# DeltaNet in a streaming encoder layer: the two tiles of a pair share one chain of small passes for norms and factors, and one for the output norm

## The chip, the cores and the metric

The kernel runs on one core of one Trainium2 chip. A core has five engines with a queue each, worked off in order: PE (TensorE, matmuls and transposes; its weight loads are listed as PEld), DVE (VectorE), ACT (ScalarE), POOL (GpSimd) and SP (SyncE, which here issues the DMAs). The metric is the device time of one execution in microseconds, as the median of the runs.

## The reference

One inference step of one encoder layer, for 2,048 new frames of one stream and for 16 frames each of eight running streams: 2,176 frames or 17 tiles of 128, the last of which (tile 16) is the sample tile. An input projection feeds three mixers: band attention, a gated DeltaNet and an S5 state space model. Their outputs go through an output projection and a feed-forward network, each with a layer norm. Only the DeltaNet (4 heads of 64) is touched. For q and k of each frame and head it needs reciprocal norms, from them six factors, a solve and a recurrence in chunks of 64 frames, and an RMS norm of the output:

```python
conv = jax.nn.silu(conv.astype(f32) + lp['b_conv_b'].astype(f32))
qb, kb, vb = jnp.split(conv, 3, axis=-1)
qb = l2_normalize(qb.reshape(bsz, t_len, B_HEADS, B_HEAD_DIM))
kb = l2_normalize(kb.reshape(bsz, t_len, B_HEADS, B_HEAD_DIM))
...
ob, s_new = gated_delta_rule(qb, kb, vb, g, beta, s0)
gate = jax.nn.silu(gate_b.astype(f32).reshape(bsz, t_len, B_HEADS, B_HEAD_DIM))
ob = ob * lax.rsqrt(jnp.mean(ob * ob, -1, keepdims=True) + RMS_EPS) * lp['b_norm_w'].astype(f32) * gate
```

## The kernel before

The first part, `mix`, runs three streams side by side. `project1` and `project2_all` are the projections: matmuls into the PSUM tile `pps`, each product in three passes (L65 to L67) of values split into a high and a low part (`xh`, `xl` for x, `wh`, `wl` for weights; the split is one copy on ACT, L60, and one subtraction on DVE, L61). `deltanet` and `s5` are the two small mixers. They are generators, and `mix` draws a step of the one or the other at a set pace. What results is a program order; the framework's scheduler then sets the order of each engine's queue from it, and hands out buffers. After `mix` come attention, the output projection and the feed-forward network.

`deltanet` goes through the tiles in pairs: (0,1) to (10,11), then the sample tile 16 alone, then (12,13) and (14,15). For each tile `b_pre` does the convolution with its SiLU (six blocks of features in `s2`, with three passes L512 and one L515 each on DVE), transposes q, k and v on PE (L528, L535), squares and sums q and k (L532), and takes the reciprocal root of the eight sums of a frame by a bit trick and three Newton steps (`rsqrt`, twelve passes of 128x8 on DVE: L343 to L350, tiles `bnt`, `bny`, `bnh`, `bns`, `bnz`). Six more passes (L544 to L549) form F, the factors of q and k. With F come `qkn` on DVE (L572) and `qdkb` on POOL (L574), `kdec` and the right-hand side R; PE transposes `qkn` (L583) and `qdkb` (L587), ACT copies them (`qknT`, `qdT`, `kbT`), and PE forms the scores (L601, into `at` and `qkT` by L603 on DVE).

For both tiles of a pair at once `b_inverse` inverts the 16x16 diagonal blocks on DVE (30 passes on `tp` and `Ti`, L625 and L627) and sends the result through memory (`tD`) into the tile `TU`. Then, tile by tile, `b_solve` (L649, L661, L669), `b_rec` (L686 to L702; two chunks, each by way of DVE) and `b_out`: square on POOL (L770), sum (L772), L773 and a second `rsqrt` of 128x4 (tiles `ont` to `onz`), `osq` (L775), two transposes on PE (L786) into the PSUM tile `brs`, and the gate (L788). `brs` has a single buffer, which the recurrence uses too; `bps`, for the transposes and scores, has two.

Of the kernel before, what the change touches and what calls it, by code (L numbers as in the profile page):

```python
# [9 lines left out]
F32 = mybir.dt.float32  # L10
# [4 lines left out]
OP = mybir.AluOpType  # L15
AX = mybir.AxisListType
# [25 lines left out]
class K:  # L42
# [88 lines left out]
    def mix(self, upto):  # L131
# [10 lines left out]
        with ExitStack() as es:  # L142
            dense = self.project1(es)
            next(dense)
            self.s5_setup()
            for _ in range(5):
                next(dense)
            self.parts_done = 1
            self.b_consts(bes)
            self.b_pools(bes)  # L150
            due = 0.0
            for i, _ in enumerate(dense):
                if i in (5, 11):
                    self.parts_done += 1
                due += PACE1 if i < 12 else PACE1B
                while due >= 1:
                    next(deltanet)
                    due -= 1
        with ExitStack() as es:
            self.merge((self.project2_all(es), 1.0), (deltanet, PACE_B), (self.s5(), PACE_C))  # L160
# [5 lines left out]
    def deltanet(self):  # L166

        gates = -1

        def ready(t):  # L170
            return self.parts_done > min(t // 6, 2)

        for t in [0, 2, 4, 6, 8, 10, 16, 12, 14]:
            n = 1 if t == 16 else 2
            while not ready(t + n - 1):
                yield 0.1
            if gates < min(t // 6, 2):
                gates += 1
                self.b_gates(gates)
            blk = self.bw.tile([32 * n, 16, 16], F32, name="blk", tag="blk", bufs=2)  # L180
            st = []
            for i in range(n):
                st.append(self.b_pre(t + i, blk, i))
                yield 1
            TU = self.b_inverse(st, blk)
            for x, (T, U) in zip(st, TU()):
                self.b_solve(x, T, U)
                o = self.bw.tile([128, 1, 4, 64], F32, name="o", tag="o", bufs=2)
                if t == 16:
                    self.b_rec_sample(x, o)  # L190
                else:
                    self.b_rec([x], o)
                self.b_out(x["t"], 1, o)
                yield 1
        self.nc.sync.dma_start(self.A["o_sp"], self.S)

    def evac(self, dst, src, scale=None):
# [273 lines left out]
    def t2(self, name, tag="pa"):  # L471
        return self.bw.tile([128, 4, 128], F32, name=name, tag=tag, bufs=5 if tag == "pa" else 1)

    def b_pre(self, t0, blk, bi):

        nc, A = self.nc, self.A
        V, mm = nc.vector, nc.tensor.matmul
        n = 1
        sam = t0 == 16
        bw, bk, bp = self.bw, self.bk, self.bp  # L480
        T = n * 128
# [5 lines left out]
        for f in range(6):  # L487
            fr = slice(f * 128, (f + 1) * 128)
            if sam:
# [5 lines left out]
                o = s2[:, f].rearrange("p (b t) -> p b t", t=16)  # L495
            else:
# [12 lines left out]
                o = s2[:, f]  # L509
# [8 lines left out]
        elif t0 + n == 16:  # L518
            nc.sync.dma_start(A["o_cvp"], cv[:, :, 0])
        qk = bw.tile([128, n, 8, 64], F32, name="qk", tag="qk", bufs=2)  # L520
        ss = bw.tile([128, n * 8], F32, name="ss", tag="ss", bufs=2)
        R = []
        for i in range(n):
            t = t0 + i
            ts = slice(i * 128, (i + 1) * 128)
            ps = bp.tile([128, 512], F32, name="bps", tag="b", bufs=2)
            for f in range(4):
                nc.tensor.transpose(ps[:, f * 128:(f + 1) * 128], s2[:, f, ts], self.ident)  # L528
            nc.scalar.copy(qk[:, i], ps.rearrange("p (h d) -> p h d", h=8))
            sq = self.t2("sq").rearrange("p a (b d) -> p (a b) d", d=64)  # L530
            nc.scalar.activation(sq, ps.rearrange("p (h d) -> p h d", h=8), AF.Square)
            V.tensor_reduce(ss[:, i * 8:(i + 1) * 8], sq, AX.X, OP.add)  # L532
            ps = bp.tile([128, 512], F32, name="bps", tag="b", bufs=2)
            for f in range(2):
                nc.tensor.transpose(ps[:, f * 128:(f + 1) * 128], s2[:, 4 + f, ts], self.ident)  # L535
            r = bk.tile([128, 4, 128], F32, name="R", tag="R")
            V.tensor_tensor(r[:, :, 0:64], ps[:, 0:256].rearrange("p (h d) -> p h d", h=4),
                            self.hbeta[:, t].unsqueeze(2).to_broadcast([128, 4, 64]), OP.mult)
            R.append(r)
        V.tensor_scalar(ss, ss, 4e-6, None, OP.add)  # L540
        rn = self.rsqrt(bw, ss, n * 8, "bn").rearrange("p (t h) -> p t h", h=8)
        F = bw.tile([128, n, 6, 4], F32, name="F", tag="F", bufs=2)
# [4 lines left out]
        V.tensor_tensor(F[:, :, 3], F[:, :, 1], self.beta[:, tt], OP.mult)  # L547
        V.tensor_tensor(F[:, :, 4], F[:, :, 3], self.egc[:, tt], OP.mult)
        V.tensor_tensor(F[:, :, 5], F[:, :, 1], self.kd[:, tt], OP.mult)  # L549
        st = []  # L550
        for i in range(n):
            t = t0 + i
# [206 lines left out]
        for p in range(2):  # L759
            nc.sync.dma_start(A["o_ss"][:, p], Sc[p])  # L760

    def b_out(self, t0, n, o):

        nc = self.nc
        V = nc.vector
        bw, bp = self.bw, self.bp
        T = n * 128
        of = o.rearrange("p t h e -> p (t h) e")
        sq = bw.tile([128, n * 4, 64], F32, name="osq", tag="po", bufs=4)
        nc.gpsimd.tensor_tensor(sq, of, of, OP.mult)  # L770
        ms = bw.tile([128, n * 4], F32, name="ms", tag="ms", bufs=2)
        V.tensor_reduce(ms, sq, AX.X, OP.add)  # L772
        V.tensor_scalar(ms, ms, 1.0 / 64, 1e-6, OP.mult, OP.add)  # L773
        rn = self.rsqrt(bw, ms, n * 4, "on")
        V.tensor_tensor(sq, of, rn.unsqueeze(2).to_broadcast([128, n * 4, 64]), OP.mult)  # L775
        g = bw.tile([128, 2, T], F32, name="gt", tag="po", bufs=4)
        gsrc, gs = self.at(self.gT, t0)
        gs = slice(gs.start, gs.start + T)
        nc.sync.dma_start(g, gsrc[:, gs].rearrange("(f p) t -> p f t", p=128))
        th = bw.tile([128, 2, T], F32, name="gth", tag="po", bufs=4)  # L780
        nc.scalar.activation(th, g, AF.Tanh, scale=0.5)
        V.scalar_tensor_tensor(g, th, 1.0, g, OP.add, OP.mult)
        ps = self.brp.tile([128, 512], F32, name="brs", tag="r")
        for f in range(2):
            for i in range(n):
                nc.tensor.transpose(ps[:, f * T + i * 128:f * T + (i + 1) * 128],  # L786
                                    sq[:, i * 4 + 2 * f:i * 4 + 2 * f + 2].rearrange("p a e -> p (a e)"), self.ident)
        V.scalar_tensor_tensor(th, ps[:, 0:2 * T].rearrange("p (f t) -> p f t", f=2), self.nw, g, OP.mult, OP.mult)  # L788
        nc.sync.dma_start(self.mixT[512:768, t0 * 128:t0 * 128 + T].rearrange("(f p) t -> p f t", p=128), th)
# [1145 lines left out]
```

## Time and profile before

| | |
|---|---|
| median of the runs | 2846.88 us (2844.42 to 2847.21, three runs) |
| the profiled execution | 2848.35 us, its span 2846.6 us |
| PE, PEld | 96%, 85% of the span busy |
| DVE, ACT, POOL | 68%, 46%, 36% |
| mean granted clock | 0.991 |
| DeltaNet's part of the span | about 130 to 760 us |

Each row of the profile is read against the engine's queue: an engine works its list in order, so a late operand holds everything behind it. A wait is put down to the instruction that released it. The page's busy shares are means over stages with different limits, so the tables by stretch matter more than they do.

### The profile page before, as it was taken

The page shows a single profiled execution, that of the slowest core. Times are in us where ns is not written, and L with a number is a line of the kernel's source. Part 1 is how long each engine was busy: PE and PEld are TensorE (multiplying, and loading weights), DVE is VectorE, ACT ScalarE, POOL GpSimd, SP SyncE. Part 2 cuts the span into 40 slices and gives each one's busy share as a digit, 9 for nine tenths or more (in the row PEclk, how much of TensorE's full clock was granted, in tenths as well). Part 3 has the DMA queues.
Part 4 walks back from the last instruction along what each step waited for, and adds up shares of the span by engine and source line. Part 5 has one row for each costly group of instructions (what it writes and reads, how often), then busy time and mean ns, then how long its engine had stood idle before and what let it go on. Part 6 is the DMA issues. An engine that isn't in the chain of part 4 may idle for free.

```text
span 2846.6 us, 46363 instructions
## 1 busy us (share of the span) xinstructions
PE 2739.7 (96%) x16685; PEld 2405.9 (85%) x16685; DVE 1947.2 (68%) x4949; ACT 1307.0 (46%) x2714; POOL 1037.4 (36%) x914
## 2 busy tenths in 40 slices
PE   8999999989989899999999999999999999999998
PEld 8988888867777677788889998989999988998897
DVE  7587888798653788878755555566556557676676
ACT  3554554343355778612334433454434335444443
POOL 0010111232221232122354454445544553676674
PEclk9999999999999999999999999999999999999999
DMA  5734445555457652156622211253222224422321
GB/s 183 208 106 118 116 114 125 151 147 155 146 147 244 207 168 61 51 199 203 231 88 65 84 60 60 74 207 119 74 74 90 89 67 165 155 91 94 119 87 55
DMA packets 293437, 355.55 MB, mean 125 GB/s; under 512 B 85699, under 2 KB 218647, under 8 KB 292887
## 3 DMA queue, kind: packets, MB, share of 16 engines
q1 hardware_dynamic: 293206, 352.59, 39.6%
q8 instruction: 131, 2.15, 0.3%
q14 instruction: 100, 0.81, 0.1%
HBM read 280.25 MB, written 74.89 MB: 125 GB/s over the span
## 4 chain that ended last, share of the span: by engine, by line
PE 71%; DVE 12%; DMA 6%; issue 4%; ACT 3%; POOL 3%; SPq 1%; DVEq 0%; ACTq 0%; POOLq 0%
PE fdp L66 8%; PE fdp L67 8%; PE fdp L65 8%; PE pps L66 3%; PE pps L67 3%; PE pps L65 3%; PE wops L65 2%; PE wops L67 2%; PE wops L66 2%; PE fupv L67 2%; PE fupv L65 2%; PE fupv L66 2%; PE fupz L67 2%; PE fupz L65 2%; PE fupz L66 2%
## 5 line engine op out<-in xcount | busy, mean ns | idle before, releaser
L1570 POOL TENSOR_TENSOR wu<-wur,wu 128x512 fp32r<-128x512 f32 x308 | 416.9, 1357 | 600.6 <-ACT wu L1569 599.6
L1693 DVE TENSOR_TENSOR fy<-fy,fdp 128x512 f32<-128x512 f32 x500 | 341.1, 685 | 255.8 <-PE fdp L67 255.6
L65 PE MATMUL fdp<-wdh,hh 128*128 128x512 f32 x1020 | 397.8, 391 | 1.6 <-DVE fy L1693 1.1
L67 PE MATMUL fdp<-wdh,hl 128*128 128x512 f32 x1020 | 397.3, 389 | 1.1 <-DVE hl L1643 1.1
L66 PE MATMUL fdp<-wdl,hh 128*128 128x512 f32 x1020 | 397.2, 389 | 0.8 <-DVE wdl L61 0.8
L1569 ACT CAST wu<-wur 128x512 fp32r<-128x512 f32 x308 | 189.5, 617 | 427.1 <-DMA wur<-in_w_upL 173.5
L65 PE MATMUL pps<-xh,wh 128*128 128x384 f32 (+2 forms) x800 | 280.4, 352 | 11.7 <-ACT xh L60 10.4
L66 PE MATMUL pps<-xl,wh 128*128 128x384 f32 (+2 forms) x800 | 279.9, 350 | 2.1 <-DVE xl L61 2.1
L67 PE MATMUL pps<-xh,wl 128*128 128x384 f32 (+2 forms) x800 | 277.6, 348 | 0.1
L65 PEld LDWEIGHTS fdp<-wdh,hh 128*128 128x128 f32 x1020 | 191.4, 188 | 42.0 <-DVE fy L1693 2.8
L67 PEld LDWEIGHTS fdp<-wdh,hl 128*128 128x128 f32 x1020 | 191.5, 188 | 41.8 <-DVE hl L1643 2.0
L66 PEld LDWEIGHTS fdp<-wdl,hh 128*128 128x128 f32 x1020 | 191.5, 188 | 39.0 <-DVE wdl L61 1.1
L1643 DVE TENSOR_TENSOR hl<-fre,hh 128x384 fp32r<-128x384 f32 (+1 forms) x180 | 145.4, 809 | 83.9 <-ACT hh L1642 83.0
L60 ACT CAST wdh<-wdr 128x1024 fp32r<-128x1024 f32 x92 | 96.6, 1051 | 204.4 <-PE fdp L67 202.7
L65 PEld LDWEIGHTS pps<-xh,wh 128*128 128x128 f32 x800 | 152.1, 191 | 24.9 <-ACT xh L60 12.8
L61 DVE TENSOR_TENSOR wl<-wr,wh 128x512 fp32r<-128x512 f32 (+1 forms) x152 | 107.2, 714 | 87.0 <-ACT wh L60 84.5
L66 PEld LDWEIGHTS pps<-xl,wh 128*128 128x128 f32 x800 | 152.1, 190 | 13.8 <-DVE xl L61 5.1
L67 PEld LDWEIGHTS pps<-xh,wl 128*128 128x128 f32 x800 | 152.1, 190 | 11.4 <-issue 1.8
L61 DVE TENSOR_TENSOR wdl<-wdr,wdh 128x1024 fp32r<-128x1024 f32 x92 | 131.6, 1436 | 11.0 <-ACT wdh L60 10.9
L60 ACT CAST wh<-wr 128x512 fp32r<-128x512 f32 (+1 forms) x152 | 92.4, 619 | 79.8 <-DMA wr<-in_w_inA 35.0
L1638 ACT ACTIVATE fre<-fre,ld_b_up 128x384 f32<-128x384 f32 (+1 forms) x144 | 86.0, 597 | 65.3 <-DVE fre L1647 43.0
L1229 ACT ACTIVATE P<-P,st 128x640 f32<-128x640 f32 (+4 forms) x128 | 97.2, 760 | 30.5 <-DVE st L1226 29.8
(577 smaller groups left out, 7250.7 us busy)
## 6 DMA issues: line engine op xcount, KB each, us to landing
wdr<-in_w_dnL SPq DMA_DIRECT2D x96, 512.0 KB
wur<-in_w_upL SPq DMA_DIRECT2D x88, 512.0 KB
wr<-in_w_inA SPq DMA_DIRECT2D x70, 512.0 KB
TU<-tD SPq DMA_DIRECT2D x34, 256.0 KB
y<-in_x SPq DMA_DIRECT2D x17, 512.0 KB
x<-y SPq DMA_DIRECT2D x17, 512.0 KB
fxr<-x SPq DMA_DIRECT2D x17, 512.0 KB
fy<-x SPq DMA_DIRECT2D x17, 512.0 KB
```

The source lines that it names most:

```text
L60: nc.scalar.copy(hi, src)
L61: nc.vector.tensor_tensor(lo, src, hi.bitcast(F32), OP.subtract)
L65: mm(out, lh, rh, start=first, stop=False, **kw)
L66: mm(out, lh, rl, start=False, stop=False, **kw)
L67: mm(out, ll, rh, start=False, stop=last, **kw)
L1229: self.nc.scalar.activation(x, x, AF.Exp, scale=-1.0, bias=st[:, q:q + 1], accum_out=st[:, 2 + q:3 + q])
L1569: self.nc.scalar.copy(hi, src)
L1570: P.tensor_tensor(lo, src, hi.bitcast(F32), OP.subtract)
L1638: nc.scalar.activation(r, src, AF.Relu, bias=self.bu[:, c * 2 + i:c * 2 + i + 1])
L1643: V.tensor_tensor(hl, r, hh.bitcast(F32), OP.subtract)
L1693: V.tensor_tensor(y, y, ps[x], OP.add)
```

## The change

`b_pre` is cut in three. `b_conv` does the convolution, the transposes and the sums of squares of one tile and writes its eight sums into its half of a shared tile `ss`. `b_factors` runs once for the pair, on 16 columns: one `rsqrt` and one set of six passes for F. The rest of `b_pre` then runs for each tile with its slice of F. In the same way `b_square` sums the squares of a tile's output into its half of a shared `ms`, `b_root` takes one reciprocal root for the pair, and `b_out` follows for both tiles after the second recurrence. A pair still yields four times, at other places. The sample tile goes through the same functions alone.

```diff
             blk = self.bw.tile([32 * n, 16, 16], F32, name="blk", tag="blk", bufs=2)
-            st = []
+            st, qr = [], []
+            ss = self.bw.tile([128, n * 8], F32, name="ss", tag="ss", bufs=2)
             for i in range(n):
-                st.append(self.b_pre(t + i, blk, i))
-                yield 1
+                qr.append(self.b_conv(t + i, ss[:, i * 8:(i + 1) * 8]))
+                if i < n - 1:
+                    yield 1
+            F = self.b_factors(t, n, ss)
+            for i in range(n):
+                st.append(self.b_pre(t + i, *qr[i], F[:, i:i + 1], blk, i))
+                if i < n - 1 or n == 1:
+                    yield 1
             TU = self.b_inverse(st, blk)
-            for x, (T, U) in zip(st, TU()):
+            os_ = []
+            ms = self.bw.tile([128, n * 4], F32, name="ms", tag="ms", bufs=2)
+            for i, (x, (T, U)) in enumerate(zip(st, TU())):
                 self.b_solve(x, T, U)
                 o = self.bw.tile([128, 1, 4, 64], F32, name="o", tag="o", bufs=2)
                 if t == 16:
                     self.b_rec_sample(x, o)
                 else:
                     self.b_rec([x], o)
-                self.b_out(x["t"], 1, o)
-                yield 1
+                os_.append((o, self.b_square(o, ms[:, i * 4:(i + 1) * 4])))
+                if i < n - 1:
+                    yield 1
+            rn = self.b_root(n, ms)
+            for i, (o, sq) in enumerate(os_):
+                self.b_out(t + i, 1, o, sq, rn[:, i * 4:(i + 1) * 4])
+            yield 1
...
-    def b_pre(self, t0, blk, bi):
+    def b_conv(self, t0, ss):
...
-        ss = bw.tile([128, n * 8], F32, name="ss", tag="ss", bufs=2)
...
+        return qk, R
+
+    def b_factors(self, t0, n, ss):
+
+        V, bw = self.nc.vector, self.bw
         V.tensor_scalar(ss, ss, 4e-6, None, OP.add)
         rn = self.rsqrt(bw, ss, n * 8, "bn").rearrange("p (t h) -> p t h", h=8)
...
+        return F
+
+    def b_pre(self, t0, qk, R, F, blk, bi):
...
-    def b_out(self, t0, n, o):
+    def b_square(self, o, ms):
+        sq = self.bw.tile([128, 4, 64], F32, name="osq", tag="po", bufs=4)
+        of = o.rearrange("p t h e -> p (t h) e")
+        self.nc.gpsimd.tensor_tensor(sq, of, of, OP.mult)
+        self.nc.vector.tensor_reduce(ms, sq, AX.X, OP.add)
+        return sq
+
+    def b_root(self, n, ms):
+        self.nc.vector.tensor_scalar(ms, ms, 1.0 / 64, 1e-6, OP.mult, OP.add)
+        return self.rsqrt(self.bw, ms, n * 4, "on")
+
+    def b_out(self, t0, n, o, sq, rn):
...
-        sq = bw.tile([128, n * 4, 64], F32, name="osq", tag="po", bufs=4)
-        nc.gpsimd.tensor_tensor(sq, of, of, OP.mult)
-        ms = bw.tile([128, n * 4], F32, name="ms", tag="ms", bufs=2)
-        V.tensor_reduce(ms, sq, AX.X, OP.add)
-        V.tensor_scalar(ms, ms, 1.0 / 64, 1e-6, OP.mult, OP.add)
-        rn = self.rsqrt(bw, ms, n * 4, "on")
         V.tensor_tensor(sq, of, rn.unsqueeze(2).to_broadcast([128, n * 4, 64]), OP.mult)
```

The scheduler makes new queues of it. Three places follow; a number behind a name tells its buffers apart, and code lines behind the change are shifted (L528 is now L541, L583 is L610).

DVE, factors of the pair (12,13). Before, tile 12 (`qkn_7813`) had them to itself, and its scores (`at_7836`) came before the sums of tile 13 (`ss_8053`):

```order
L549 TENSOR_TENSOR F_7796<-F_7796,b4_kd_1398 128x4
L572 TENSOR_TENSOR qkn_7813<-qk_7762,F_7796 128x512
L548 TENSOR_TENSOR F_7796<-F_7796,b4_egc_1397 128x4
L577 TENSOR_TENSOR kdec_7818<-qk_7762,F_7796 128x256
L603 TENSOR_TENSOR at_7836<-bps_7838,DT_7803 128x2x64
L603 TENSOR_TENSOR qkT_7837<-bps_7838,DM_7804 128x2x64
L603 TENSOR_TENSOR at_7836<-bps_7849,DT_7803 128x2x64
L603 TENSOR_TENSOR qkT_7837<-bps_7849,DM_7804 128x2x64
L537 TENSOR_TENSOR R_8066<-bps_8063,b4_hbeta_1394 128x4x64
L532 TENSOR_REDUCE ss_8053<-sq_8060 128x8
```

Now F is 2x4 wide and both tiles follow it (`qkn_7746` is tile 12, `qkn_7807` tile 13), with convolution passes of tile 14 (`s2_8394`) around:

```order
L565 TENSOR_TENSOR F_7729<-F_7729,b4_beta_1393 128x2x4
L567 TENSOR_TENSOR F_7729<-F_7729,b4_kd_1398 128x2x4
L599 TENSOR_TENSOR qkn_7746<-qk_7493,F_7729 128x512
L566 TENSOR_TENSOR F_7729<-F_7729,b4_egc_1397 128x2x4
L604 TENSOR_TENSOR kdec_7751<-qk_7493,F_7729 128x256
L604 TENSOR_TENSOR kdec_7812<-qk_7696,F_7729 128x256
L599 TENSOR_TENSOR qkn_7807<-qk_7696,F_7729 128x512
L526 SCALAR_TENSOR_TENSOR s2_8394<-cin_8423,ld_b_cw_1358,s2_8394 128x128
```

So tile 12's `qkn` moved behind the sums of both tiles, and tile 13's directly behind it.

PE, the same pair. Before, tile 13's transposes (`s2_7996`) came after tile 12's scores, and tile 13's own `qkn` 43 projection matmuls later:

```order
L786 MATMUL brs_7534<-ld_c_ident_92,osq_7506 128x128 x2
...
L583 MATMUL bps_7823<-ld_c_ident_92,qkn_7813 128x128 x4
L587 MATMUL bps_7829<-ld_c_ident_92,qdkb_7815 128x128 x4
...
L528 MATMUL bps_8054<-ld_c_ident_92,s2_7996 128x128 x4
...
L535 MATMUL bps_8063<-ld_c_ident_92,s2_7996 128x128 x2
...
L583 MATMUL bps_8113<-ld_c_ident_92,qkn_8103 128x128 x4
L587 MATMUL bps_8119<-ld_c_ident_92,qdkb_8105 128x128 x4
```

Now tile 13's transposes (`s2_7640`) stand ahead of the sample tile's output (`osq_7237`), and the two tiles' `qkn` six projection matmuls apart:

```order
L541 MATMUL bps_7697<-ld_c_ident_92,s2_7640 128x128 x4
L548 MATMUL bps_7706<-ld_c_ident_92,s2_7640 128x128 x2
...
L818 MATMUL brs_7264<-ld_c_ident_92,osq_7237 128x128 x2
...
L610 MATMUL bps_7756<-ld_c_ident_92,qkn_7746 128x128 x4
L614 MATMUL bps_7762<-ld_c_ident_92,qdkb_7748 128x128 x4
...
L610 MATMUL bps_7817<-ld_c_ident_92,qkn_7807 128x128 x4
...
L614 MATMUL bps_7823<-ld_c_ident_92,qdkb_7809 128x128 x4
```

So tile 13's transposes moved up by 50 projection matmuls, tile 12's `qkn` down by 8.

DVE, the splits `xl` of the first x of `project2_all`, which PE needs for its next product. Before, the factor chain of tile 14 (`bnz_8785`, `bns_8784`) ran between them:

```order
L61 TENSOR_TENSOR xl50_8614<-xr_8615,xh50_8613 128x512
L625 TENSOR_TENSOR tp_8155<-blk_7699,Ti_8154 64x48
L350 SCALAR_TENSOR_TENSOR bnz_8785<-bns_8784,bnz_8785 128x8
L959 TENSOR_TENSOR WB_9119<-st1_428,pr_400 128x256
L627 TENSOR_TENSOR Ti_8154<-Ti_8154,tp_8155 64x12x4
L348 TENSOR_TENSOR bns_8784<-bnz_8785 128x8
L963 TENSOR_TENSOR ZC_9117<-ZC_9117,tz_9118 128x544
L625 TENSOR_TENSOR tp_8155<-blk_7699,Ti_8154 64x55
L349 TENSOR_TENSOR bns_8784<-bns_8784,bnh_8783 128x8
L512 SCALAR_TENSOR_TENSOR s2_8950<-cin_8952,ld_b_cw_1358,s2_8950 128x128
```

Now it is the convolution of tile 15 (`s2_8549`):

```order
L61 TENSOR_TENSOR xl50_8299<-xr_8300,xh50_8298 128x512
L652 TENSOR_TENSOR tp_7859<-blk_7429,Ti_7858 64x28
L529 SCALAR_TENSOR_TENSOR s2_8549<-th_8588,s2_8549 128x128
L654 TENSOR_TENSOR Ti_7858<-Ti_7858,tp_7859 64x2x14
L1010 TENSOR_TENSOR Kt_8497<-Kt_8497,ld_s5_dI_367 16x2x16
L526 SCALAR_TENSOR_TENSOR s2_8549<-cin_8591,ld_b_cw_1358,s2_8549 128x128
L652 TENSOR_TENSOR tp_7859<-blk_7429,Ti_7858 64x15
L526 SCALAR_TENSOR_TENSOR s2_8549<-cin_8601,ld_b_cw_1358,s2_8549 128x128
L654 TENSOR_TENSOR Ti_7858<-Ti_7858,tp_7859 64x15
L526 SCALAR_TENSOR_TENSOR s2_8549<-cin_8591,ld_b_cw_1358,s2_8549 128x128
```

So between the splits small passes of 8 columns left, and convolution passes of 128 columns and more of the inverse moved up.

## Rows read from the trace of the kernel before

**Rows 1.** The page, part 1: busy time, share and instructions of each engine.
```profile
PE 2739.7 (96%) x16685; PEld 2405.9 (85%) x16685; DVE 1947.2 (68%) x4949; ACT 1307.0 (46%) x2714; POOL 1037.4 (36%) x914
```

**Rows 2.** Busy time of each engine by stretch; first the stretch and its length.
```profile
core 0: us, PE busy (x) PEld busy (x) DVE busy (x) ACT busy (x) POOL busy (x), PEclk, DMA share, GB/s
200.00:300.00 100.00, 96.45 (x692) 84.72 (x692) 81.05 (x326) 46.35 (x119) 13.82 (x16) 1.00 0.39 109
...
500.00:560.00 60.00, 58.20 (x460) 51.75 (x458) 43.60 (x151) 23.98 (x63) 11.97 (x26) 1.00 0.52 146
560.00:586.00 26.00, 25.68 (x158) 20.13 (x159) 18.94 (x62) 6.54 (x15) 9.34 (x22) 1.00 0.32 113
586.00:634.00 48.00, 35.65 (x261) 27.94 (x258) 45.23 (x158) 25.18 (x62) 19.28 (x26) 0.89 0.59 164
634.00:700.00 66.00, 64.58 (x460) 52.76 (x460) 60.55 (x200) 23.11 (x52) 18.07 (x28) 1.00 0.54 152
700.00:760.00 60.00, 56.25 (x333) 43.57 (x332) 38.69 (x112) 18.87 (x39) 8.60 (x15) 0.97 0.45 131
```

**Rows 3.** DVE's groups by shape, 0 to 800 us: count, busy us, mean ns.
```profile
L512 DVE SCALAR_TENSOR_TENSOR s<-cin,ld_b_cw,s 128x128 f32<-128x128 f32 x288 | 100.4, 365 | 3.5 <-ACT s L510 2.4
...
L548 DVE TENSOR_TENSOR F<-F,b_egc 128x4 f32<-128x4 f32 x17 | 10.4, 613 | 0.1
L349 DVE TENSOR_TENSOR bns<-bns,bnh 128x8 f32<-128x8 f32 x51 | 8.5, 166 | 0.3
L349 DVE TENSOR_TENSOR ons<-ons,onh 128x4 f32<-128x4 f32 x51 | 8.5, 166 | 0.1
```

**Rows 4.** DVE in order of time: start us, duration us, line, operation.
```profile
374.28 0.33 DVE L512 SCALAR_TENSOR_TENSOR s<-cin,ld_b_cw,s 128x128 f32<-128x128 f32 x1
374.54 0.15 DVE L544 TENSOR_SCALAR F<-bnz 128x4 f32<-128x4 f32 x1
374.61 0.15 DVE L545 COPY F<-bnz 128x4 f32<-128x4 f32 x1
...
375.77 1.01 DVE L548 TENSOR_TENSOR F<-F,b_egc 128x4 f32<-128x4 f32 x1
```

**Rows 5.** PE's waits from 0 to 560 us: total us, times, longest.
```profile
PE brs L786 <- DVE Ti L627: 2.7, 3, 1.5
PE bps L583 <- DVE qkn L572: 2.5, 3, 1.3
PE bps L587 <- POOL qdkb L574: 2.0, 6, 1.0
...
PE bps L583 <- DVE F L548: 0.6, 1, 0.6
```

**Rows 6.** Busy time from the sample tile's last update to the last split.
```profile
578.00:623.00 45.00, 36.48 (x247) 29.88 (x246) 40.76 (x149) 20.75 (x48) 17.12 (x23) 0.89 0.50 139
```

**Rows 7.** PE in order of time: two projection matmuls.
```profile
590.13 0.34 PE L65 MATMUL pps<-xh,wh 128*128 128x384 f32 x1
590.31 0.34 PE L66 MATMUL pps<-xl,wh 128*128 128x384 f32 x1
```

**Rows 8.** PE's waits from 586 to 634 us.
```profile
PE bps L535 <- DVE s L515: 3.8, 1, 3.8
PE bps L587 <- POOL qdkb L574: 2.2, 2, 2.0
PE bps L528 <- DVE qkT L603: 1.7, 1, 1.7
PE bps L601 <- ACT kbT L590: 1.3, 2, 0.8
```

**Rows 9.** Busy time from 600 to 620 us.
```profile
600.00:620.00 20.00, 15.67 (x60) 11.37 (x60) 19.18 (x56) 9.43 (x18) 9.29 (x11) 0.74 0.67 191
```

**Rows 10.** The chain that ended last, at the last pair's inverse.
```profile
698.51 3.63 DMA tD<-Ti
702.20 3.08 DMA TU<-tD
```

More of the change, by code (lines that the diff above doesn't have):

```diff
@@ L549, in b_pre @@
         V.tensor_tensor(F[:, :, 5], F[:, :, 1], self.kd[:, tt], OP.mult)
+        return F
+    def b_pre(self, t0, qk, R, F, blk, bi):
+        nc = self.nc
+        V, mm = nc.vector, nc.tensor.matmul
+        n = 1
+        sam = t0 == 16
+        bw, bk, bp = self.bw, self.bk, self.bp
         st = []
```

## The prediction

> **What bounds the kernel now.** I read the page first, then busy time by stretch, then who waits for whom on PE and on DVE, then DVE's instructions in order of time. The page [rows 1] shows PE busy for 96% of the span; no other engine is above 85%. So a change of DVE's work is worth only what PE idles for it. The table by stretch [rows 2] says where that is. From 200 to 560 us PE is busy 96 to 97% while DVE has work for 73 to 81% of the time: PE bounds it, and DVE's passes lie beside matmuls. From 586 to 634 us it is the other way round: DVE 45.23 of 48 us, PE 35.65, so PE idles 12.4 us and waits for DVE. After it, PE is at 98%, and from 700 to 760 us at 94%. Only DeltaNet's stretch, about 130 to 760 us, is touched. Behind it PE's order is word for word the old one: the last 9,703 of its 13,017 listed rows agree, only with other line numbers. I count that tail as a pure shift.
>
> **What goes.** A pair of tiles ran two factor chains (19 instructions: L540, twelve in `rsqrt`, six for F) and two output chains (13: L773 and twelve). Now it runs one of each: 32 fewer per pair, 256 for the eight pairs; the sample tile, alone, keeps its 32. Width costs nothing that the rows can show: the 8-wide and the 4-wide pass both last 166 ns [rows 3]. The price of one is the distance between starts, not its duration: where independent passes follow each other, they start 70 ns apart though each lasts 0.15 us [rows 4]. With a little for dependent ones I take 75 ns, and 256 x 0.075 = 19 us of DVE's queue. By durations it would be 256 x 0.166 = 42 us; the starts are the nearer row, since what follows can begin then. The Trainium skill (VectorE: DVE Perf Modes, section The DRAIN you can't avoid) says that the next operation does not start until the pipe is empty; by that the 42 us would count, and the rows at 374.54 and 374.61 do not agree. The one exception stands in the rows too: L548, a four-wide pass, lasts 1.01 us at 375.77 and 613 ns in the mean [rows 3, 4], because POOL reads for `qdkb` just then. One such pass per pair goes, a half us each.
>
> **What it is worth, in time order.** The sum is made against the profiled execution, 2848.35 us (its span 2846.6); it stands 1.5 us above the median of the runs, 2846.88.
>
> (a) Before 560 us the passes are covered by matmuls; if that cover went, the whole 19 us would be on the path. What is not covered is PE's waits at the ends of these chains: 2.7 us where the output transpose (L786) comes, 2.5 us for `qkn`, 2.0 us for `qdkb`, 0.6 us for F: 7.8 us [rows 5]. (The first is put down to `Ti`, which stands beside the output chain in DVE's queue.) One chain of two goes, so 3.9 us; but the one that stays waits for the second tile, so I take **-3.0** (ends 0 and -7.8).
>
> (b) The stretch where DVE bounds. The point that lets PE go on is the last of the eight splits `xl` of the first x of `project2_all`. I count DVE's list from the sample tile's last state update to that split: 148 rows become 147, but others. Out go 37 small passes (37 x 0.075 = 2.8 us), one `qkn` (0.6) and one collision of L548 (0.5). In come 20 passes of the convolution of tile 15 (20 x 0.3 = 6.0, between 0.26 us from its start to the next at 374.28 us [rows 4] and its mean of 365 ns [rows 3]), 15 of the block inverse (15 x 0.13 = 2.0) and S5 passes of 0.8 us. Net +4.9 on 40.76 us, in a piece that took 45 us [rows 6]: DVE idled 4.2 us there, mostly for the transposes and scores of tiles 12 and 13, and now has convolution passes for that time. So the split would end 45.7 us after the start instead of 45, and the start itself comes earlier: 12 projection matmuls fewer stand ahead of it on PE, 0.18 us from start to start [rows 7], 2.1 us. Together **-1.5** (ends -4.9 with the idle time wholly used and less work in front, +4.9 if neither helps). Of PE's waits in this stretch [rows 8], 2.2 us for POOL's `qdkb` and 1.3 us for `kbT` fall behind or beside that split; DVE has tile 15's convolution behind it there already, and I let **-2** of them go (0 to -3.5). The 3.8 and 1.7 us on the transposes of tile 14 are inside the DVE path counted before; they move to x, they do not go twice.
>
> (c) The granted clock is 0.74 between 600 and 620 us [rows 9], that is some 10 us at 1.2 instead of 2.4 GHz, around the waits of 1.7 and 3.8 us; 5.2 us of full clock. PE waits for DVE for much of it, so I take **-1** (0 to -5.2).
>
> (d) Right after the split the new order packs the solve of tile 13, the recurrence of tile 12 and the scores of tile 14 with hardly a projection matmul between, where seven stood before. PE idles 1.4 us from 634 to 700 now [rows 2]; I double some of that: **+1** (0 to +3).
>
> (e) For the last pair PE waits for the inverse to come back through memory, 3.63 and 3.08 us one after the other [rows 10]. The two DMAs are not touched; the passes ahead of them lose a few neighbours and PE has less to do meanwhile: 0 (-1.8 to +2).
>
> (f) POOL and ACT issue the same instructions as before; SP's queue has the same transfers, only in another order: 0. The joined output chains need no further buffer wait on PE than the one on the single buffer `brs`, four or five matmuls apart: 0.
>
> Sum -3.0 - 1.5 - 2 - 1 + 1 = -6.5: 2841.85 us profiled, **2840.4 us** as the median of the runs. By the durations (42 us in place of 19) term (b) would lose 6.1 instead of 2.8 us to small passes, and the sum would be 2837 us.
>
> **The rivals.** First, *no change*: all of it is hidden. For it speaks that PE is at 96% up to 560 us, and that the work taken from the DVE stretch is replaced by convolution passes that come earlier. Then (a) is 0, (b) is near 0, and the time is 2846 us. Against it: PE does wait at these chains' ends, and DVE does bound 48 us.
>
> Second, *slower*: the first tile of a pair now waits for the second's convolution. Before, tile 12's factors, `qkn` and scores ran while tile 13 was still being convolved; now both stand behind both convolutions, and tile 15's convolution stands ahead of the x splits. Place: DVE between 578 and 623 us. Price: the net +4.9 us of (b) if the 4.2 us of idle time stay, and 2 us of (d): 2846.9 + 6 = 2853 us. It decides once the work put ahead of the last x split exceeds 4.2 + 2.1 = 6.3 us; I count 4.9. The Trainium skill (Perfetto Trace Analysis, section Optimizing Scalar/DVE Operations) advises the reverse of this change where an engine is not saturated and yet causes bubbles: break instructions up, so that work is completed sooner. In the stretch before 560 us the rows agree with its condition, since DVE is not full there; from 586 us on it is full, and there fewer passes should win.
>
> Third, that the change does not do what it says: the order of the built program shows eight chains of 16 and eight of 8 columns in place of 16 each, so that is out.
>
> **How the numbers follow.** Measurement can tell about 0.2%, 5.7 us, from no change. The forecast gets 0.55 and reaches by itself from 2832 to 2845; of those 13 us, 9.2 lie beyond the bound, so 0.39 of it counts as faster and 0.16 as the same. No change: 0.25 (0.23 same, 0.02 faster). Slower: 0.18 (0.16 slower, 0.02 same). Another 0.02 is for a mishap at the pools, slower. That makes 0.41 faster, 0.41 the same, 0.18 slower. The low end takes in (a) at its full 7.8, (b) at 1.5 and its waits' 3.5, and the clock's whole 5.2, 18 us below the median: 2829 us. The high end is the slower rival: 2853 us.
>
> **What would show it.** DVE about 20 us less busy by starts, some 40 us by summed durations. PE's waits at the output transposes, at `qkn` and at F half as long. At tile 14's transposes no wait of 3.8 us, the half clock near 601 us gone or shorter; the last x split within 2 us of where it was, counted from the sample tile's last update. From 760 us on, the same gaps as now, all shifted alike. I am wrong if PE's idle time moves to the x splits or to the packed piece after them, if the early waits stay at some 8 us, or if the tail does not shift as a whole.

## The result, and the profile after

The changed kernel takes 2858.97 us (median of five runs, 2856.85 to 2866.89); the kernel before, beside it, 2844.42 us. The ratio is 1.0055 (95% interval 1.0042 to 1.0068): slower by 14.5 us, where I had forecast 6.5 us faster (2840.4 against 2846.9) and a range up to 2853. The profiled execution is the slowest of the five, 2866.89 us (span 2865.1), 18.5 us above the one profiled before.

The page's first part, as [rows 1]:

```profile
PE 2741.4 (96%) x16685; PEld 2407.6 (84%) x16685; DVE 1934.9 (68%) x4693; ACT 1305.2 (46%) x2714; POOL 1035.4 (36%) x914
```

The 256 DVE instructions are gone, and DVE is 12.3 us less busy, 48 ns for each. PE does the same work; its busy time grows by 1.7 us, and the rest of the 18.5 us is time in which PE idles. The table by stretch, as [rows 2]:

```profile
200.00:300.00 100.00, 96.53 (x721) 82.72 (x720) 79.85 (x267) 46.46 (x119) 15.51 (x18) 1.00 0.39 106
500.00:560.00 60.00, 58.34 (x456) 51.46 (x455) 44.15 (x163) 26.50 (x74) 8.05 (x10) 1.00 0.54 148
560.00:586.00 26.00, 20.73 (x143) 19.45 (x141) 18.89 (x52) 6.08 (x17) 11.81 (x38) 0.93 0.46 145
586.00:634.00 48.00, 35.20 (x245) 27.85 (x245) 39.47 (x124) 21.14 (x50) 19.72 (x23) 0.89 0.42 121
634.00:700.00 66.00, 61.07 (x424) 46.98 (x423) 56.67 (x169) 25.99 (x61) 18.29 (x28) 0.99 0.52 151
700.00:760.00 60.00, 58.26 (x376) 48.46 (x374) 41.56 (x114) 15.95 (x33) 7.37 (x14) 0.96 0.44 126
```

By the clock these stretches no longer hold the same work. So I added up PE's matmuls, each at the median duration that its form had before, and took the time at which each kernel had done the same sum. By that the change is behind by some 1 us at 231 us of the old time, 9 at 412, 15 at 531, 22 at 641, 21 at 788, at 1194 and at 2203, and 18.5 at the end. The loss is made between 230 and 680 us, most of it in the stretch that I had called covered; behind that there is a shift, the same to within 3 us. Up to 531 us half of it is waiting and half is the clock, as the same work shows, first in the kernel before, then in the change:

```profile
130.00:531.00 401.00, 385.38 (x2985) 342.85 (x2983) 325.60 (x1336) 201.24 (x526) 61.15 (x76) 1.00 0.45 118
130.00:546.00 416.00, 392.62 (x2987) 346.98 (x2985) 320.68 (x1146) 200.92 (x527) 60.66 (x77) 0.98 0.44 114
```

PE idles 23.4 us in place of 15.6, and its clock, which was granted in full before, stands at the lower of its two levels (1.2 in place of 2.4 GHz) for 13.6 us, from 186, 330 and 456 us on: 6.8 us of full clock.

PE's waits from 0 to 560 us, as [rows 5]:

```profile
PE bqs L676 <- DVE R L688: 5.2, 7, 1.7
PE brs L818 <- DVE osq L807: 4.0, 4, 1.4
PE bps L541 <- DVE s L529: 3.7, 6, 1.6
PE bps L610 <- DVE qkn L599: 2.2, 3, 0.9
...
PE bps L614 <- POOL qdkb L601: 0.4, 2, 0.2
```

At `qkn` and `qdkb` the waits are shorter, as forecast. But the solve, which waited 1.2 us for its passes R, now waits 5.2 us for them, and PE's transposes of q and k wait 3.7 us for the convolution. One such place on DVE, in order of time:

```profile
453.94 0.17 DVE L562 TENSOR_SCALAR F<-bnz 128x8 f32<-128x8 f32 x1
...
454.38 0.69 DVE L599 TENSOR_TENSOR qkn<-qk,F 128x512 f32<-128x512 f32 x1
454.98 1.00 DVE L566 TENSOR_TENSOR F<-F,b_egc 128x8 f32<-128x8 f32 x1
455.91 0.41 DVE L604 TENSOR_TENSOR kdec<-qk,F 128x256 f32<-128x256 f32 x1
456.25 0.67 DVE L688 TENSOR_TENSOR R<-R,bqs 128x512 f32<-128x512 f32 x1
```

The joined chain, `qkn` and `kdec` stand in the queue ahead of the solve's R; PE, which has the next product of that solve at the head of its own queue, idles 1.68 us. And where x's splits come:

```profile
PE s5p L1001 <- DVE WB L996: 9.6, 1, 9.6
```

The new order puts S5's transposes of WB ahead of x's matmuls on PE, and on DVE WB's last pass behind a convolution and part of the inverse: 9.6 us, where tile 14's transposes cost 3.8 and 1.7 us before [rows 8].

### The profile page after: what moved, and what is told of

It reads as the page before. It is cut to its first block, busy times and chain, and to the rows that moved or that the text cites. A ratio compares the mean times of both kernels' runs of the same rounds, so it can differ in the third digit from the quotient of the medians.

```text
span 2865.1 us, 46134 instructions
## 1 busy us (share of the span) xinstructions
PE 2741.4 (96%) x16685; PEld 2407.6 (84%) x16685; DVE 1934.9 (68%) x4693; ACT 1305.2 (46%) x2714; POOL 1035.4 (36%) x914
## 4 chain that ended last, share of the span: by engine, by line
PE 73%; DVE 11%; DMA 6%; ACT 4%; issue 3%; POOL 2%; SPq 1%; DVEq 0%; ACTq 0%; POOLq 0%
PE fdp L65 8%; PE fdp L66 8%; PE fdp L67 8%; PE pps L67 3%; PE pps L65 3%; PE pps L66 3%; PE bqs L676 2%; PE fupv L65 2%; PE fupv L67 2%; PE fupv L66 2%; PE fupz L67 2%; PE fupz L66 2%; PE fupx L66 2%; PE fupx L67 2%; PE fupz L65 2%
## 5 line engine op out<-in xcount | busy, mean ns | idle before, releaser
L65 PEld LDWEIGHTS pps<-xh,wh 128*128 128x128 f32 x800 | 152.1, 191 | 24.9 <-ACT xh L60 13.5
```

The source lines that it names most:

```text
L65: mm(out, lh, rh, start=first, stop=False, **kw)
```

## The experiments

### One half of the change, and its order

Only the norms joined (e1), only the outputs joined (e2):

```diff
 # e1, against the change
-                os_.append((o, self.b_square(o, ms[:, i * 4:(i + 1) * 4])))
+                sq = self.b_square(o, ms)
+                self.b_out(t + i, 1, o, sq, self.b_root(1, ms))
 # e2, against the change
-            F = self.b_factors(t, n, ss)
...
+                q = self.b_conv(t + i, ss)
+                st.append(self.b_pre(t + i, *q, self.b_factors(t + i, 1, ss), blk, i))
```

> Only the chain of norms and factors is shared by the pair (both convolutions, then one set of factors, then the rest tile by tile); each tile keeps its own output norm right behind its recurrence, and its own output transposes. Before is 2844.4 us, the change 2859.0. Theory A (the first tile's scores wait for the second tile's convolution and the second tile's scores are put in one step with the inverse and the first solve, so that PE has less to do beside them): nearly the whole loss, 2855 to 2860 us. Theory B (the joined output: both tiles' output transposes stand back to back behind one root): no loss, 2840 to 2846 us. Theory C (any new order of the queues costs some 10 us): 2850 to 2860 us here and in every other run.

2869.1 us, ratio 1.0082 (1.0058 to 1.0106); its six runs lie between 2854.8 and 2880.5.

> Only the chain of the output norm is shared by the pair; convolution, factors and scores go tile by tile as before. Theory A (the loss is in the joined norms and factors): 2840 to 2846 us. Theory B (the loss is in the joined output, whose transposes L818 gather 4.7 us of PE's waits from 195 to 560 us and 4.1 us after that, where 3.4 and 0.4 stood): 2850 to 2858 us. Theory C (any new order costs): 2850 to 2860 us.

2859.4 us, 1.0051 (1.0039 to 1.0063). Each half alone costs as much as both, or more. The first is 9 us above A's and C's ranges; the second lies in C's range and 1.4 us above B's. So A's and B's signs hold, each in its run, and neither of the two can be the whole cause.

The change's order with the chains apart (e3), and its sharing with the yields where they were (e4):

```diff
 # e3
-            F = self.b_factors(t, n, ss)
+                F.append(self.b_factors(t + i, 1, ss[:, i * 8:(i + 1) * 8]))
-            rn = self.b_root(n, ms)
+            rn = [self.b_root(1, ms[:, i * 4:(i + 1) * 4]) for i in range(n)]
 # e4
                 qr.append(self.b_conv(t + i, ss[:, i * 8:(i + 1) * 8]))
-                if i < n - 1:
-                    yield 1
...
-                if i < n - 1 or n == 1:
-                    yield 1
+                yield 1
```

> The order of the change and its yields, but without sharing: behind both convolutions each tile runs its own chain of factors, and behind both recurrences its own root, 256 small passes more than the change, as many as before. Theory of order (the loss is from where the work stands, the passes are hidden): 2855 to 2865 us, as slow as the change or up to 6 us slower. Theory of sharing itself (wide passes, a shared tile for the sums): the time of before, 2844 us.

2863.3 us, 1.0063 (1.0050 to 1.0076): slow without any sharing.

> All that the change shares, but the yields of a pair put back to where they stood in the program before: after the first tile's scores, after the second tile's, after the first recurrence, after the outputs, so that the inverse and the first solve are in a step of their own again; both convolutions are in the first step. Theory Y (the change's pace: its third step holds the second tile's scores, the inverse and the first tile's solve at once, and PE waits for the solve's passes, R L688, 3.3 us against 0.9 before): the loss goes, 2838 to 2848 us. Theory A (the first tile waits for the second's convolution, wherever the yields stand): 2855 to 2862 us.

2869.5 us, 1.0082 (1.0069 to 1.0095). Y falls, and the time is above A's range too: the yields are not the cause, and this order is worse than the change's.

### Early and late pairs

Each is the change under a condition on `t`, with the old code in the other branch: `t < 12` (e5) and `t >= 12` (e6).

> Shared chains only in the pairs (0,1) to (10,11), which end about 530 us; the sample tile and the pairs (12,13) and (14,15) go tile by tile as before. In the profiled runs the change falls behind by 15.7 us of its 21 before 531 us. Theory E (the loss is made in the early pairs and adds up pair by pair): 2853 to 2857 us. Theory L (the loss is the late stretch, above all the 9.6 us that PE waits for S5's WB at L1001): 2844 to 2848 us. Theory C (any other order of the queues costs some 15 us, wherever the edit stands): 2855 to 2865 us.

2863.0 us, 1.0057 (1.0044 to 1.0069).

> The complement: shared chains only in the pairs (12,13) and (14,15); up to the sample tile the queues are those of before. Theory E (early pairs): 2846 to 2851 us. Theory L (late stretch): 2855 to 2860 us. If the two losses add up to that of the change (14.5 us), this run and the one before stand 14 to 15 us above before together; theory C: 2855 to 2865 us for each.

2851.0 us, 1.0017 (1.0009 to 1.0026). Most of the loss comes with the early pairs; L falls. C's number holds in e5 and falls in e6, E's the other way round. The two add up to 21 us, not 14.5.

### The same work in another order

Two Newton steps in place of three (a less precise root), and one line moved:

```diff
 # e7, against the kernel before
-        for _ in range(3):
+        for _ in range(2):
 # e8, against the kernel before: two lines moved up, ahead of qkn
+            kd = bk.tile([128, 4, 64], F32, name="kdec", tag="kdec")
+            V.tensor_tensor(kd, qk[:, i, 4:8], fb(5, 4), OP.mult)
             qkn = self.t2("qkn")
```

> The kernel before, tile by tile, with two Newton steps in rsqrt in place of three (a reciprocal root of less precision): 102 small passes of DVE fewer, nothing joined, no yield moved, but the scheduler forms another order of the queues from it. Theory of the passes (a pass that goes is worth 75 ns where DVE holds PE up): 2840 to 2844 us. Theory C (an order other than before's costs, even with less work in it): 2855 to 2865 us.

2859.9 us, 1.0048 (1.0036 to 1.0061): 102 passes less, nothing joined, and 13.5 us slower.

> The kernel before with one line moved: kdec (0.4 us on DVE) is formed ahead of qkn instead of behind qdkb and R. No pass goes or comes, nothing is joined; the orders of the queues differ from before's in few places and only from about the last third of this stage on. Theory C (any other order costs): 2850 to 2860 us. Theory of the joined chains (only their order costs): 2843 to 2847 us, at most 17 x 0.4 us later in qkn, of which matmuls hide nearly all.

2845.5 us, 0.9996 (0.9987 to 1.0005). C in its strict form falls: an order that is new in few places costs nothing. The next four change nothing but the order of the six blocks:

```diff
 # e9 and e10 against the kernel before, e11 and e12 against the change
-        for f in range(6):
+        for f in (2, 3, 0, 1, 4, 5):      # e9, e11; (4, 5, 0, 1, 2, 3) in e10, e12
```

> The kernel before, nothing joined and no pass gone, but the convolution takes its six blocks of features in another order: k, q, v in place of q, k, v. The work is the same piece for piece; the scheduler forms other queues from it (444 lines of difference in PE's list; 942 for v first; 941 between before and the change). Theory C (an order that the scheduler forms anew costs 10 to 20 us against before's, whatever the edit): 2853 to 2865 us. Theory of the joined chains (what costs is that the two tiles' work stands behind one another's): 2843 to 2848 us.

2853.1 us, 1.0034 (1.0022 to 1.0046).

> The same with the blocks of v first (v, q, k). Theory C: 2853 to 2865 us. Theory of the joined chains: 2843 to 2848 us.

2863.2 us, 1.0074 (1.0062 to 1.0086). Both lie in C's range.

> The changed kernel, all shared, with the blocks of the convolution in the order k, q, v. Theory C: within some 8 us of the change (2859), on either side, and against the kernel before with the same order of blocks no slower, or faster by the 4.4 us that sharing was worth at the change's own order (2863.3 without, 2859.0 with). Theory of the joined chains: 10 to 15 us slower than before with the same order of blocks.

2869.4 us, 1.0077 (1.0062 to 1.0092).

> The changed kernel with the blocks in the order v, q, k. The same expectations, against the kernel before with v first.

2868.3 us, 1.0088 (1.0075 to 1.0101). The same work, instruction for instruction, costs 9.6 and 19.7 us more in another order. On the same order of blocks the joined kernel is 16.3 and 5.1 us slower than the separate one, so neither of my two expectations for it held. In these two pairs of runs joining costs something beyond the shuffle; but each joined kernel is a new order too, and at the change's own places for the work it is the separate chains (e3) that are slower, by 4.4 us, though the intervals overlap. So a price of joining by itself is not shown by them.

Busy time by stretch, 130 to 560 and 560 to 700 us, first of the kernel before, then of e10, then of e7:

```profile
130.00:560.00 430.00, 412.81 (x3182) 366.87 (x3180) 347.13 (x1401) 212.46 (x553) 71.44 (x99) 1.00 0.46 121
560.00:700.00 140.00, 125.91 (x871) 100.83 (x871) 124.72 (x419) 54.83 (x127) 46.69 (x75) 0.96 0.52 149
```

```profile
130.00:560.00 430.00, 404.95 (x3080) 361.21 (x3079) 330.85 (x1357) 206.27 (x540) 68.32 (x79) 0.98 0.44 112
560.00:700.00 140.00, 121.66 (x816) 97.27 (x814) 114.83 (x387) 53.17 (x126) 52.30 (x87) 0.91 0.51 153
```

```profile
130.00:560.00 430.00, 410.66 (x3136) 364.48 (x3135) 336.74 (x1310) 209.91 (x550) 70.49 (x83) 0.98 0.45 116
560.00:700.00 140.00, 120.71 (x822) 95.94 (x820) 115.81 (x383) 51.67 (x122) 51.77 (x86) 0.91 0.49 143
```

PE idles more in both stretches, and the granted clock is lower in both. In e10 a single wait, at `qkn`, takes 7.4 us:

```profile
PE bps L583 <- DVE qkn L572: 12.4, 8, 7.4
PE bps L587 <- POOL qdkb L574: 8.4, 9, 1.9
```

### The order held still

For the last six a table fixes each engine's queue, the whole of it in f1, f2 and f5, and in f3, f4 and f6 all but the joined steps; only ordering edges are added, no waits. No run holds the unchanged kernel in its own order, so the price of the table itself is not measured; f1 and f2, below before and level with it, say that it is a few us at most.

```diff
+        for a, b in zip(seq, seq[1:]):
+            tc.add_manual_dep(b, a.name, ...NoSync...)
```

> Two Newton steps in rsqrt in place of three (a reciprocal root of less precision), as in the earlier run with two steps (2859.9 us), but with each engine's queue held to the order of the kernel before by a table: PE, ACT, POOL and SP have its lists line for line, DVE its list without the 102 passes. Theory C (the new order cost the 13.5 us, not the passes): 2838 to 2845 us, and the difference to before is the price of the passes themselves, 102 of them at 17 to 75 ns, 1.7 to 7.7 us. If the loss came with the missing passes in any order: 2855 to 2862 us.

2841.5 us, 0.9983 (0.9974 to 0.9992): 4.1 us faster than before, 18 us faster than e7, the same program in the scheduler's order. If the table costs nothing, this is the price of a pass when nothing else moves: 40 ns (22 to 73 by the interval). It rests on the medians; the profile does not place the gain, since at equal PE work f1 is 2.3 us ahead at 700 us, not at all at 788, and 8.7 at the end, where nothing was changed.

> Only the output norm is shared, as in the earlier run of that (2859.4 us), but in the order of the kernel before: the pair's one root stands where the second tile's stood, the first tile's osq, output transposes and store stand right ahead of the second's, those of the second six projection matmuls later where nothing else needs brs; the gate is loaded with the squares, and its buffers (po) are five in place of four. All else keeps its place. Theory C: 2838 to 2846 us, 104 passes at 17 to 75 ns (1.8 to 7.8 us) less whatever the back-to-back transposes take. Theory B (the joined output itself costs): 2850 to 2860 us.

2847.3 us, 1.0005 (0.9996 to 1.0014), against 2859.4 us for the same sharing in the scheduler's order. B falls, and C's range is missed by 1.3 us: the joined output is free here, and worth nothing either, though its 104 passes at the 40 ns of f1 would be 4 us.

> The reverse: nothing is shared, but PE, ACT, POOL and SP have the lists of the changed kernel line for line, and DVE has them with each joined chain replaced by the two tiles' chains one behind the other in its places (the first tile's osq ahead of the second's root). Against the change (2859.0 us) this adds 256 small passes and nothing else. If passes are hidden in that order too: 2857 to 2861 us; at 17 ns each 2863 us; at my 75 ns 2878 us.

2913.4 us, 1.0231 (1.0217 to 1.0245), 54 us above the change, 213 ns for each of the 256 passes. PE's waits from 130 to 700 us:

```profile
PE brs L819 <- DVE gth L821: 17.5, 5, 4.8
PE bqs L677 <- DVE R L689: 15.6, 8, 5.3
...
PE bps L611 <- DVE F L568: 8.8, 2, 4.9
```

The change's order fits its own short chains: with longer ones in the same places PE stands at the outputs (`gth`), at the solve (R) and at the factors (F). But e3 has the same instructions as f5 in the order that the scheduler forms for them, and takes 2863.3 us. So sharing is worth much in this one order and at most some 4 us against e3, and an order that was made for other chains can by itself cost some 50 us.

Next the norms joined (f3), and everything joined (f4), with the order of before for all that does not hang on the chains:

> Only the norms and factors are shared (as in the earlier run of that, 2869.1 us), but everything except the pairs' factor chains and what each tile does with its factors keeps, on each engine, the order of the kernel before by a table; the factor chains and those steps (qkn, qdkb, R, kdec, their transposes, the scores, 904 instructions in all) are put in by the scheduler where they become ready. PE's list then differs from before's by 160 lines in place of 979. Theory C (the reordering of all else costs): 2838 to 2848 us. Theory A (the first tile of a pair waits for the second's convolution, in any order): 2850 to 2860 us.

2878.2 us, 1.0112 (1.0095 to 1.0129): 33 us slower. C falls here; A's sign holds, at three times its price.

> The changed kernel, all shared, in the same manner: all but the factor chains, the steps that use the factors, the squares, roots and outputs of the pairs (1168 instructions) keeps the order of the kernel before; PE's list differs from before's by 194 lines in place of 941. Theory C: 2836 to 2848 us, no more than the change's 256 passes fewer are worth (256 at 40 ns, as with two Newton steps in the old order, are 10 us) below before. Theories A and B (joined chains cost wherever they stand): 2852 to 2862 us.

2889.2 us, 1.0156 (1.0141 to 1.0171), 44 us slower and above every range. The change has the same instructions in the scheduler's order and is 14.5 us slower, so some 30 of the 44 us are what this held order costs. At equal PE work f3 is 4.5 us behind at 168 us and some 23 at 231 us, over the pair (0,1). Its waits from 130 to 240 us, and its busy time by stretch, the second being the one that holds the work of 168 to 231 us of before:

```profile
PE bqs L671 <- DMA TU<-tD: 3.4, 1, 3.4
PE bps L536 <- DVE s L524: 2.8, 1, 2.8
```

```profile
140.00:170.00 30.00, 24.80 (x226) 23.05 (x225) 22.43 (x75) 16.85 (x47) 7.63 (x8) 1.00 0.37 94
172.50:253.40 80.90, 68.04 (x426) 59.06 (x426) 53.38 (x204) 34.45 (x89) 9.53 (x12) 0.86 0.32 87
```

The same work in the kernel before, and its wait at the solve from 130 to 235 us:

```profile
140.00:170.00 30.00, 27.66 (x239) 26.01 (x238) 25.66 (x95) 18.97 (x56) 8.90 (x9) 1.00 0.47 122
168.00:231.00 63.00, 58.90 (x427) 51.05 (x427) 50.98 (x212) 32.60 (x82) 9.30 (x11) 1.00 0.38 106
PE bqs L649 <- DMA TU<-tD: 1.0, 1, 1.0
```

Both tiles' scores come late, so the inverse returns late, and PE stands at the solve (3.4 us against 1.0). The longest wait of the stretch is another, at the output transposes:

```profile
250.80 0.17 DVE L647 TENSOR_TENSOR tp<-blk,Ti 64x15 f32<-64x15 f32 x1 [6.27 <-DMA blk<-aD]
251.31 0.41 DVE L802 TENSOR_TENSOR osq<-o,onz 128x256 f32<-128x256 f32 x1
251.78 0.69 PE L813 MATMUL brs<-ld_c_ident,osq 128*128 128x128 f32 x2 [5.01 <-DVE osq L802]
```

By the table the first pass of the next inverse (`tp`) stands on DVE ahead of the last steps of an output root that is not joined at all. The joined factors bring that inverse later, DVE idles 6.3 us for its operand, and PE 5.0 us behind it. So part of f3's 33 us is made by the table, which leaves steps standing behind one that the joining delays. Last, the norms joined only in the four pairs (4,5) to (10,11):

> As the run with joined norms in the old order (2878.2 us), but joined only in the pairs (4,5) to (10,11), where PE has projection matmuls beside DeltaNet; the pairs (0,1), (2,3), (12,13) and (14,15) go tile by tile. In that run 24 of the 33 us came before 290 us of the old time, at the first pairs, and 10 more from 591 to 679 us, at the last two; between 290 and 531 us it fell 5 us further behind. If the wait of the first tile for the second's convolution costs only where PE has nothing else to do: 2840 to 2848 us (76 passes fewer at 40 ns are 3 us). If it costs in every pair: 2851 to 2860 us.

2850.3 us, 1.0025 (1.0014 to 1.0035). The time lies between my two ranges, but they were counted from 2845.3 us, and before stands at 2843.2 beside this run: the ratio on 2845.3 gives 2852.4 us, in the second range. So joining in the held order costs in the covered pairs too, 1.8 us for each of the four. If the pairs add up, the other four have 6.5 us each in the mean ((33 - 7) / 4), very unevenly, since the pair (0,1) alone has some 18.

## Why the prediction was wrong

Two steps failed. The first is the frame of the sum: I took passes out of an order and let the rest stand, with a changed order only in (b) and (d). The scheduler forms the queues anew from the first pair on, and a new order of the same work alone cost 9.6 and 19.7 us (e9, e10), more than the whole sum of -6.5. The second is the price that (a) put on the wait of the first tile for the second: 0.9 us (-3.0 in place of -3.9) for all pairs before 560 us. Where the rest does stand, the change is not faster either but 44 us slower (f4), with the norms alone 33 (f3), 24 of them before 290 us of the old time. Both figures hold losses that the table makes, so they are not the price of that wait alone. And the waits beside the new chains before 560 us, for R and for the convolution, were in no term.

- **The price of a pass**, 75 ns. In a held order it is 40 ns, the upper end of the interval just short of mine; DVE's busy time says 48 ns. Where PE waits for the chain itself a pass costs far more (213 ns in f5). There is no one price. "A little for dependent ones" was a wrong reading: the rows below, of the kernel before, show passes of which each needs the one ahead of it. They start 0.2 us apart (the median of 29 such neighbours in that trace is 200 ns, of 61 neighbours that do not need each other 73 ns). So a pass in a chain that PE waits for can cost 0.2 us, near the 213 ns of f5, and one whose gaps other passes fill far less.
- **The 166 ns and the width.** The rule that I had set beside my price from the Trainium skill (VectorE: DVE Perf Modes, section The DRAIN you can't avoid), that the next operation waits for the empty pipe, I had read without the sentence beside it, by which an operation that is not held starts earlier. So it does not make the whole 166 ns count, and the 40 ns of f1 are far from them. That width is free nearly held: a pass of the factors' `rsqrt` lasts 189 ns in the mean at 16 columns and 173 at 8.

```profile
580.73 0.16 DVE L349 TENSOR_TENSOR bns<-bns,bnh 128x8 f32<-128x8 f32 x1
580.92 0.17 DVE L350 SCALAR_TENSOR_TENSOR bnz<-bns,bnz 128x8 f32<-128x8 f32 x1
581.12 0.17 DVE L348 TENSOR_TENSOR bns<-bnz 128x8 f32<-128x8 f32 x1
```

- **(a)**, -3.0 for shorter waits at the chains' ends. At `qkn` and `qdkb` they fell from 4.5 to 2.6 us; at the output transposes they rose from 3.5 to 4.7 us, and R and the convolution made new ones. PE's idle time up to 531 us of the old time grew by 8.3 us, outside my ends of 0 and -7.8. "Covered" was true of the old order only.
- **(b)**, -1.5 and -2. The waits for `qdkb` and `kbT` went to 0.2 us each, and tile 14's went; the 9.6 us at WB took their place. I had the last split 0.7 us later after the sample tile's last update: it is 4.5 us later (595.0 to 644.5 us, 49.5 in place of 45.0 [rows 6]), near my upper end. The update itself I had 2.1 us earlier; it is 17 us later, for the loss before it.
- **(c)**, -1 for the clock. The stretch has the same 0.89, and others got worse: 0.93 from 560 to 586 us, where it was 1.00, and the 6.8 us before 531 us, where I had no term for the clock.
- **(d)**, +1: the work of 634 to 700 us of before stands from 656 to 723 us now, and PE idles 3.0 us in it in place of 1.4, near what I took. But its clock there is 0.95 in place of 1.00, another 3.4 us.
- **(e), (f)** held as far as the waits show (1.0 us for the last pair's inverse in place of 1.8), and the tail is a shift to within 3 us.
- **The slower rival** had the right sign and half the cause: the first tile does wait for the second's convolution. Its place was wrong, since f3 loses first at the pair (0,1) and not only from 578 us on, and so was its price, 6 us against 14.5 in the change and 33 in the held order; for the late pairs alone (e6, 4.5 us) it was near. The Trainium skill's advice that I quoted for it (Perfetto Trace Analysis, section Optimizing Scalar/DVE Operations: break instructions up where an unsaturated engine makes bubbles) agrees in sign with f3 and f6, before 560 us, where DVE is not full.

What the runs show, then. Joining the outputs is neutral (f2). Joining the norms costs 33 us if all else keeps its order (f3), part of it the table's. The scheduler's new order for the joined kernel avoids some 30 of the 44 us of f4, but a new order costs something itself: with the chains apart, new orders stand 9.6, 13.5, 17.3 and 19.7 us above before (e9, e7, e3, e10), with all joined 14.5, 23.4, 24.8 and 25.9 (the change, e4, e12, e11). The two groups overlap, and how the change's 14.5 us divide between order and joining can't be said: the parts do not add up. Also open is what makes the order of before better than these; I found no single place, only more waits of 1 to 10 us on DVE.

The one kernel that is faster than before is f1, by 0.17%, with a less precise root; with the full computation none is.

## What to carry to other kernels

Where a scheduler forms the queues, an edit that adds, drops or moves work early in a stage is a new draw of the whole order: here that alone moved the time by 10 to 20 us (e9, e10), more than the edit could be worth, and by nothing where few places differed (e8). Before an edit is judged, hold the old order, or try a neutral shuffle of the same work beside it; but a held order also charges the edit with every step that the table leaves standing behind a delayed one (f3, f5). And of two chains that share their passes, ask who waits for the earlier one: in the old order the joined outputs could wait (f2), the joined norms ahead of an inverse could not (f3, f6).

## What I had not expected of the hardware

A wait can cost more than its length, since the granted clock falls behind it. In f3 the clock goes to the lower of its two levels (1.2 in place of 2.4 GHz) for 6.8 us from 185.9 us on, right behind the 3.4 us that PE idled at the solve. From 172.5 to 253.4 us PE idles 12.9 us where it idled 4.1 for the same work, 8.8 us more, and the mean clock is 0.86 in place of 1.00: at the lower level for 0.28 of 80.9 us, which takes away some 11 us, more than the added idle time itself. The spread of e1's runs goes with the clock as well: 2854.8 us at a mean clock of 0.991, 2880.5 us at 0.982; that is some 51 us more at the lower level, 26 us of work. Only one of these runs has a profile, so which waits set it off in the others is not shown.
